# Opening the feed-forward stage's pools ahead of the last residual, and computing two of its early products there

## The chip, the cores and the metric

The kernel runs on one core of a Trainium2 chip. The metric is the device time of one execution in microseconds (us), taken as the median of several executions. All work is in float32; TensorE is fed with float32r operands.

## The reference, cut to what matters

One diffusion block over 512 latent tokens of width 1024 (with 256 context tokens that only feed the scan). The change lies where the first half of the block ends and the second begins:

```python
mix = branch_merge(h, o_lat, z, sc_p, fn_u, ..., w_gate, b_gate, w_o)   # ends in merged @ w_o
x = x + g1 * mix
x = x + g2 * swiglu(modulate(x, norm2_g, sh2, sc2), w_ffn_in, w_ffn_out)
return rmsnorm(x, final_g)

def rmsnorm(t, gain):
    return t * rsqrt(mean(t * t, axis=-1) + 1e-6) * gain
def modulate(t, gain, shift, scale):
    return rmsnorm(t, gain) * (1 + scale) + shift
def swiglu(h, w_ffn_in, w_ffn_out):
    a, b = split_cols(h @ w_ffn_in, (2816, 2816))
    return (silu(a) * b) @ w_ffn_out
```

`w_o` is 1024 x 1024, `w_ffn_in` 1024 x 5632, `w_ffn_out` 2816 x 1024. `setup_inputs()` draws all of them from normal distributions.

## The kernel before, in words

**Splitting.** A float32 operand is split into a high part (a rounding to float32r, on ScalarE, L143) and a low part (the rest, on VectorE, L144). Every product is then three matmuls: high by high, high by low, low by high. Weights come in pieces of 128 x 1024 elements (512 KB): `load_w` (L136) issues the DMA on SyncE's queue into the buffer `wf` (three of them), `prep_w` (L146) splits the piece into `wh` and `wl` (two of each), or into tiles that are handed in as `dst`.

**The `w_o` product** (`gemm_tm`, L975) keeps four token tiles `m` of 128 tokens in eight PSUM banks. The first weights go through all four tiles; the last four pieces (three of them split into `ex0`, `ex1`, `ex2`, one held in `wh`/`wl`) are kept, and with them the tiles are finished one after the other. As each tile is done, the loop at L1059 adds it to the stream `xr` (`residual`, L1002: an addition on VectorE for each 512 columns, a square with a sum on ScalarE, a square root and a reciprocal), scales it to `xn` (L1061), transposes it on TensorE (eight 128 x 128 transposes, L1071), and applies gain and shift (L1075, L1077).

**The feed-forward input** `h @ w_ffn_in` is done in 2 x 2 blocks with seven products instead of eight (a Strassen scheme). The normed tokens are the blocks B11, B21 (tokens 0 to 255, the two halves of the contraction) and B12, B22 (tokens 256 to 511); `sums_b` (L1038) makes from them T1, T2, T3 and minus B22, and L1140 makes T4. They lie, split, in `ob` (and `obt`, `ob4`). The 2816 columns go in 11 groups `g` of 256. In a group, one `prod` (L1101) is 24 matmuls of 256 columns. Weights for the seven products are single pieces of `w_ffn_in` or sums of pieces: two of the sums are made by the DMA itself, which loads one piece (`load_w2`, SyncE's queue) and accumulates another onto it (`acc_w`, GpSimd's queue); in the list of a group these are `t` and `w`. The next sums are made on VectorE (`add_w`, L1115).

For the first three groups the two products that only need B11 and B21 are taken ahead of the loop (`ahead`, `ahead2`, L1124 to L1139), so that TensorE has work while T1 to T4 are still being made. In order, TensorE does: B11 by the pieces of groups 0, 1, 2; B21 by the pieces of groups 0, 1, 2; then, for each group, T1, T2, T3, minus B22, T4 (and B11, B21 from group 3 on).

**What sets the order.** The program is written as Python and a scheduler puts the instructions of each engine in a row by priority; each engine works its row in order. Loads and splits under `prio("prep")` stand as early as their place in the row allows. A tile waits for the last use of whatever lay in its memory. Pools open and close as a stack: `pF` (L810) serves the stage before and holds, among others, the tiles of the norm (`xn`, `h2f`, `tb`); `pG` (L1089), the pool of the feed-forward stage with `ws`, `Gq`, `tmps`, opens where `pF` closes, after the last residual. The sum `w` of every group lies in `ws`, the sum `t` in one of two places in `c16` (`pre`). Two of the three results of the early products are kept in `e01`, which is one of the three `wf` buffers (L1134).

Of the kernel before, what the change touches and what calls it, by code (L numbers as in the profile page):

```python
# [74 lines left out]
def body(tc, I, out):  # L75
# [3 lines left out]
    with es:  # L79
# [806 lines left out]
        uus = [pF.tile([128, 512], F32, name="uu", tag=t_, bufs=2) for t_ in ("u", "u", "gt", "gt")]  # L886
        for t_, p_ in zip(uus, pus[0] + pu2):
            A.copy(out=t_, in_=p_)
        def fourier(g):
            uu = uus[g]  # L890
            eo = pF.tile([128, 2, 256], F32, name="eo", tag="eo", bufs=2)
            V.tensor_tensor(out=eo[:, 0], in0=uu[:, 1:257], in1=uu[:, 511:255:-1], op=ALU.add)
            V.tensor_tensor(out=eo[:, 1], in0=uu[:, 1:257], in1=uu[:, 511:255:-1], op=ALU.subtract)
            up = pF.tile([128, 2, 2, 2, 128], F32R, name="up", tag="dng" if g % 2 else "up")
# [26 lines left out]
        for j2 in range(4):  # L921
            gt = [pF.tile([128, 512], F32, name="gt", tag="gt", bufs=2) for _ in range(2)]
# [6 lines left out]
        dnh = [pF.tile([128, 4, 512], F32, name="dng", tag=t_) for t_ in ("up", "dng")]  # L929
# [95 lines left out]
        xn = pF.tile([128, 2, 1024], F32, name="xn", tag="dng")  # L1025
# [33 lines left out]
        for m, ps in gemm_tm(I["w_o"][0], g1b, lambda k, ms: (mh[:, k, ms], ml[:, k, ms]), 8, extra, 1):  # L1059
            rs_ = residual(ps, xr, m, [xn[:, m % 2, 512 * n:512 * n + 512] for n in range(2)])  # L1060
# [3 lines left out]
            for k4 in range(2):  # L1064
                px = dbank()
                p3 = px.rearrange("p (k j) -> p k j", k=4)
                h3 = Bf[:, 4 * k4:4 * k4 + 4, js] if m < 2 else pF.tile([128, 512], F32, name="h2f", tag=("u", "gt")[m - 2], bufs=2).rearrange("p (k j) -> p k j", k=4)
# [16 lines left out]
        fstack.close()  # L1084
# [4 lines left out]
        pG = es.enter_context(tc.tile_pool(name="pG", bufs=1))  # L1089
        OB["T4"] = pG.tile([128, 2, 4, 256], F32R, name="ob4")  # L1090
        tmps = pG.tile([128, 7, 512], F32, name="tmps")
        e1g, e5, u2, e57, c22, c21, c12 = (tmps[:, i] for i in range(7))
        Gq = [pG.tile([128, 2, 512], F32, name="Gq", tag=f"Gq{i}") for i in range(11)]
        ws = [pG.tile([128, 4, 256], F32, name="ws", tag=f"ws{i}") for i in range(2)]
        third = [pG.tile([128, 4, 256], F32R, name="w3", tag=f"w3{i}") for i in range(2)]
        turn = itertools.count()
        prep3 = lambda w_: prep_w(w_, dst=third if next(turn) % 3 == 2 else None)
        wfi = I["w_ffn_in"][0].rearrange("(k p) f -> p k f", p=128)
        wsrc = lambda i, half, g: wfi[:, 4 * half:4 * half + 4, 2816 * i + 256 * g:2816 * i + 256 * g + 256]

        def prod(bank, w, b, first, last):  # L1101

            for q in range(2):
                o, cs = bank[:, 256 * q:256 * q + 256], slice(128 * q, 128 * q + 128)
                for kk in range(4):
                    mm = ((w[0], b[:, 0]), (w[0], b[:, 1]), (w[1], b[:, 0]))
                    for i, (l_, r_) in enumerate(mm):
                        T.matmul(o, lhsT=l_[:, kk, cs], rhs=r_[:, kk], start=first and q == kk == i == 0,  # L1108
                                 stop=last and kk == 3 and i == 2, skip_group_check=True)

        def acc_w(w, src):
            with prio("prep"):
                GP.dma_start(out=w, in_=src, accum_op=ALU.add)

        def add_w(w, other):  # L1115
            with prio("prep"):
                V.tensor_tensor(out=w, in0=w, in1=other, op=ALU.add)  # L1117
# [101 lines left out]
```

## Time and profile before

| | |
|---|---|
| median of the three runs shown | 964.57 us (960.88 to 968.45) |
| the profiled execution | 965.04 us |
| its span, first to last instruction | 963.2 us |
| TensorE busy | 939.9 us, 98% of the span |
| VectorE, ScalarE busy | 649.3 us, 467.9 us |
| last `w_o` matmuls to the regular rhythm of the groups | about 599.3 to 648.2 us of the span |

Times in the rows are microseconds from the start of the span. In a row of the timeline the columns are start, duration, engine, line, operation, output and inputs with shapes, count, and in brackets the idle time of the engine just before and what ended it. PE is TensorE's matmuls, DVE VectorE, ACT ScalarE, POOL GpSimd, SPq and POOLq the queues that issue DMAs. TensorE's operations overlap, so the duration of a row is longer than the step from one to the next.

### The profile page before, as it was taken

What the parts mean: (1) busy time and instruction counts of PE and PEld (TensorE: products, weight loads), DVE (VectorE), ACT (ScalarE), POOL (GpSimd) and SP (SyncE); (2) the same over time, 40 slices, a digit from 0 to 9 for tenths busy, and PEclk for the clock granted to TensorE, in tenths of its full rate; (3) what the DMA queues carried; (4) which work ended last, traced back from release to release, by engine and by line L of the source; (5) the groups of instructions that cost most, each with busy time, mean ns of one, the idle gap of its engine ahead of it and who ended that gap; (6) DMA issues with size and microseconds to landing.
All of it is one profiled execution on the core that took longest, in us unless ns stands there. A gap on an engine that the chain in (4) does not pass through costs nothing.

```text
span 963.2 us, 16357 instructions
## 1 busy us (share of the span) xinstructions
PE 939.9 (98%) x6660; PEld 807.7 (84%) x6660; DVE 649.3 (67%) x1002; ACT 467.9 (49%) x793; POOL 57.2 (6%) x69
## 2 busy tenths in 40 slices
PE   8999999999999999999999999799999999999997
PEld 7588887777788888888888888699999999988885
DVE  2585888378755423788874876778777777855575
ACT  5354885687673334362234336644444444422334
POOL 1002300000000000000000010112111110000000
PEclk9999999999999999999999999899999999999999
DMA  9920653521202232837774471689887774333332
GB/s 319 307 66 3 146 131 88 133 67 34 67 2 66 88 110 66 310 109 256 264 247 141 127 194 42 160 217 262 180 195 190 185 187 104 117 88 109 89 88 87
DMA packets 117434, 135.84 MB, mean 141 GB/s; under 512 B 18748, under 2 KB 104624, under 8 KB 117360
## 3 DMA queue, kind: packets, MB, share of 16 engines
q1 hardware_dynamic: 97168, 117.93, 39.2%
q0 software_dynamic: 13248, 14.98, 9.5%
q10 hardware_dynamic: 6944, 1.91, 0.8%
q8 instruction: 52, 0.85, 0.4%
q14 instruction: 22, 0.18, 0.1%
HBM read 131.02 MB, written 3.77 MB: 140 GB/s over the span
## 4 chain that ended last, share of the span: by engine, by line
PE 76%; DVE 9%; DMA 6%; ACT 6%; issue 2%; POOL 0%; SPq 0%; DVEq 0%; ACTq 0%
PE g L1108 17%; PE g L256 10%; PE g L257 10%; PE g L255 10%; PE d L256 5%; PE d L255 5%; PE d L257 5%; PE d L1108 3%; DVE wl L144 2%; DMA wm<-in_w_mod_dram 2%; DMA ws<-in_w_ffn_in_dram 1%; DVE acc L835 1%; DMA wf<-in_w_o_dram 1%; ACT wh L143 1%; ACT SJ L718 1%
## 5 line engine op out<-in xcount | busy, mean ns | idle before, releaser
L144 DVE TENSOR_TENSOR wl<-wf,wh 128x1024 fp32r<-128x1024 f32 x114 | 139.1, 1222 | 93.1 <-ACT wh L143 92.2
L143 ACT CAST wh<-wf 128x1024 fp32r<-128x1024 f32 x114 | 119.6, 1050 | 161.1 <-PE g L256 98.2
L255 PE MATMUL g<-hh,wh 128*128 128x512 f32 x368 | 145.6, 396 | 0.0
L257 PE MATMUL g<-hh,wl 128*128 128x512 f32 x368 | 145.3, 395 | 0.1
L256 PE MATMUL g<-hl,wh 128*128 128x512 f32 x368 | 145.2, 395 | 0.0
L1108 PE MATMUL g<-ob,wh 128*128 128x256 f32 x640 | 118.7, 287 | 3.8 <-ACT wh L143 3.8
L1108 PEld LDWEIGHTS g<-ob,wh 128*128 128x128 f32 x640 | 101.6, 195 | 4.5 <-ACT wh L143 4.5
L1108 PE MATMUL g<-ob,wl 128*128 128x256 f32 x320 | 91.6, 287 | 0.5 <-DVE wl L144 0.5
L257 PEld LDWEIGHTS g<-hh,wl 128*128 128x128 f32 x368 | 69.2, 188 | 14.5 <-issue 0.5
L256 PEld LDWEIGHTS g<-hl,wh 128*128 128x128 f32 x368 | 69.2, 188 | 13.6 <-issue 0.2
L255 PEld LDWEIGHTS g<-hh,wh 128*128 128x128 f32 x368 | 69.2, 188 | 13.6 <-issue 0.2
L1108 PEld LDWEIGHTS g<-ob,wl 128*128 128x128 f32 x320 | 62.3, 195 | 0.8 <-DVE wl L144 0.8
L835 DVE SCALAR_TENSOR_TENSOR acc<-wm,ct,acc 128x1024 f32<-128x1024 f32 x32 | 41.0, 1282 | 14.7 <-DMA acc<-in_b_mod_dram 7.6
L1108 PE MATMUL g<-ob,w 128*128 128x256 f32 x360 | 45.9, 283 | 0.2 <-issue 0.2
L1108 PEld LDWEIGHTS g<-ob,w 128*128 128x128 f32 x360 | 44.3, 192 | 0.4 <-issue 0.4
L143 ACT CAST gs<-Gq 128x512 fp32r<-128x512 f32 x22 | 13.4, 622 | 63.5 <-PE d L256 63.5
L143 ACT CAST wh<-c 128x1024 fp32r<-128x1024 f32 x21 | 22.0, 1048 | 37.0 <-DVE c L1117 19.5
L144 DVE TENSOR_TENSOR gs<-Gq,gs 128x512 fp32r<-128x512 f32 x22 | 15.0, 690 | 29.1 <-ACT gs L143 29.1
L154 DVE TENSOR_TENSOR wf<-wf,g2b 128x1024 f32<-128x1024 f32 x22 | 26.9, 1222 | 8.5 <-DMA wf<-in_w_ffn_out_dram 8.5
L255 PE MATMUL d<-wh,gs 128*128 128x512 f32 x80 | 31.1, 389 | 0.0
L257 PE MATMUL d<-wh,gs 128*128 128x512 f32 x80 | 31.1, 389 | 0.0
L256 PE MATMUL d<-wl,gs 128*128 128x512 f32 x80 | 31.1, 389 | 0.0
(481 smaller groups left out, 2078.3 us busy)
## 6 DMA issues: line engine op xcount, KB each, us to landing
wm<-in_w_mod_dram SPq DMA_DIRECT2D x48, 512.0 KB, 5.7
wf<-in_w_ffn_in_dram SPq DMA_DIRECT2D x39, 512.0 KB, 4.8
wf<-in_w_in_dram SPq DMA_DIRECT2D x31, 512.0 KB, 3.8
wf<-in_w_gate_dram SPq DMA_DIRECT2D x24, 512.0 KB, 3.8
wf<-in_w_ffn_out_dram SPq DMA_DIRECT2D x22, 512.0 KB, 3.6
c<-in_w_ffn_in_dram SPq DMA_DIRECT2D x11, 512.0 KB, 6.3
c<-in_w_ffn_in_dram POOLq DMA_DIRECT2D x11, 512.0 KB, 6.6
ws<-in_w_ffn_in_dram SPq DMA_DIRECT2D x11, 512.0 KB, 3.8
```

The source lines that it names most:

```text
L143: A.copy(out=hi, in_=f)
L144: V.tensor_tensor(out=lo, in0=f, in1=hi.bitcast(F32), op=ALU.subtract)
L154: V.tensor_tensor(out=w, in0=w, in1=scale, op=ALU.mult)
L255: T.matmul(ps, lhsT=lh, rhs=rh, start=start, stop=False)
L256: T.matmul(ps, lhsT=lh, rhs=rl, start=False, stop=False)
L257: T.matmul(ps, lhsT=ll, rhs=rh, start=False, stop=stop)
L718: A.activation(out=S[:, u ^ par, h], in_=S[:, u ^ par, h], func=AF.Copy, scale=eGl[:, u, c_:c_ + 1])
L835: V.scalar_tensor_tensor(out=acc, in0=w, scalar=ct[:, k, 0:1], in1=acc, op0=ALU.mult, op1=ALU.add)
L1108: T.matmul(o, lhsT=l_[:, kk, cs], rhs=r_[:, kk], start=first and q == kk == i == 0, stop=last and kk == 3 and i == 2, skip_group_check=True)
```

## The change

- The tiles of the second norm and of the step before it (`xn`, `h2f`, `tb`, and `uu`, `eo`, `gt`, half of `dng`) move from `pF` to a pool of their own, `pE`, on the other side of the memory.
- With these out of `pF`, `pF` closes and `pG` opens inside the loop over the `w_o` tiles, when the matmuls of the last tile (m = 3) have been written down and before its residual.
- At that place the first two early products (B11 by the pieces of groups 0 and 1) are written down, ahead of the last residual. The weights of group 0 go to `wh`/`wl`; those of group 1 are split into the place of minus B22 in `ob`, which is written only later in `sums_b`. The early result of group 2 stays behind the loop.
- The early results are kept in `tmps` (nine slices in place of seven); `e01` is gone.
- Group 0's two sums are both made in `pre`, which is loaded well ahead. From then on even groups have both sums in `pre`, odd groups both in `ws`. Before, `t` was in `pre` and `w` in `ws` for all groups.
- `pE` closes after the loop; `pG2` opens in its place for the last three `Gq` tiles and `third`.

```diff
+        estack = ExitStack()
+        pE = estack.enter_context(tc.tile_pool(name="pE", bufs=1, side="right"))
...
-        xn = pF.tile([128, 2, 1024], F32, name="xn", tag="dng")
+        xn = pE.tile([128, 2, 1024], F32, name="xn", tag="dng")
...
+        def sums_w(g, lower, left):
+
+            load_w2(wsrc(1, 0, g), lower)
+            acc_w(lower, wsrc(1, 1, g))
+            load_w2(wsrc(0, 0, g), left)
+            acc_w(left, wsrc(1, 0, g))
+
+        sums_w(0, *pre)
...
         for m, ps in gemm_tm(I["w_o"][0], g1b, lambda k, ms: (mh[:, k, ms], ml[:, k, ms]), 8, extra, 1):
+            if m == 3:
+
+                fstack.close()
+                pG = es.enter_context(tc.tile_pool(name="pG", bufs=1))
+                OB["T4"] = pG.tile([128, 2, 4, 256], F32R, name="ob4")
+                tmps = pG.tile([128, 9, 512], F32, name="tmps")
+                ws = [pG.tile([128, 4, 256], F32, name="ws", tag=f"ws{i}") for i in range(2)]
+                Gq = [pG.tile([128, 2, 512], F32, name="Gq", tag=f"Gq{i}") for i in range(8)]
+
+                Xs = [gbank() for _ in range(2)]
+                for g, dst in enumerate((None, (OB["nB22"][:, 0], OB["nB22"][:, 1]))):
+                    prod(Xs[g], prep_w(load_w(wsrc(0, 0, g)), dst=dst), OB["B11"], True, False)
             rs_ = residual(ps, xr, m, [xn[:, m % 2, 512 * n:512 * n + 512] for n in range(2)])
...
-        fstack.close()
-        pG = es.enter_context(tc.tile_pool(name="pG", bufs=1))
...
+        estack.close()
+        pG2 = es.enter_context(tc.tile_pool(name="pG2", bufs=1, side="right"))
+        Gq += [pG2.tile([128, 2, 512], F32, name="Gq", tag=f"Gq{i}") for i in range(8, 11)]
+        third = [pG2.tile([128, 4, 256], F32R, name="w3", tag=f"w3{i}") for i in range(2)]
...
-        e01 = stg.tile([128, 4, 256], F32, name="e01", tag="wf", bufs=3).rearrange("p a b -> p (a b)")
-        e1s = [e01[:, 0:512], e01[:, 512:1024], e1g]
+        e1a, e1b, e1g, e5, u2, e57, c22, c21, c12 = (tmps[:, i] for i in range(9))
+        e1s = [e1a, e1b, e1g]
         EARLY = 3
-        Xs = [ahead(g, e1s[g]) for g in range(EARLY)]
+        for g in range(2):
+            A.copy(out=e1s[g], in_=Xs[g])
+        Xs.append(gbank())
+        prod(Xs[2], prep_w(load_w(wsrc(0, 0, 2))), OB["B11"], True, False)
+        A.copy(out=e1s[2], in_=Xs[2])
...
         for g in range(11):
-            t, w = pre[g % 2], ws[g % 2]
-            load_w2(wsrc(1, 0, g), t)
-            acc_w(t, wsrc(1, 1, g))
-            load_w2(wsrc(0, 0, g), w)
-            acc_w(w, wsrc(1, 0, g))
+            t, w = (pre, ws)[g % 2]
+            if g:
+                sums_w(g, t, w)
```

What stands in an engine's row moves as follows. Up to the first residual nothing moves on any engine. ScalarE's row just ahead of the residual of tile m = 0, before (`wh` is the high part of the last `w_o` piece and of group 0's piece; the two `xn` rows are the squares of the residual):

```order
L143 CAST ex_5306<-wf 128x1024
L143 CAST ex_5308<-wf 128x1024
L143 CAST wh<-wf 128x1024 x2
L1009 ACTIVATE xn,n_s<-xr 128x512 x2
L1011 ACT_TABLE_LOAD
L1011 ACTIVATE n_r<-n_r,eps 128x1
```

and now (`ob` is the place of minus B22, `wf` here group 1's piece):

```order
L143 CAST ex_5309<-wf 128x1024
L143 CAST ex_5311<-wf 128x1024
L143 CAST wh<-wf 128x1024 x2
L143 CAST ob<-wf 128x1024
L1011 ACTIVATE xn,n_s<-xr 128x512 x2
L1013 ACT_TABLE_LOAD
L1013 ACTIVATE n_r<-n_r,eps 128x1
```

One cast has come in ahead of the first residual, and on VectorE likewise its low part, ahead of the first two additions to `xr`.

TensorE's row at the end of the `w_o` product, where the transposes of tile m = 3 stand (`cp`, `xn`), before, with buffer numbers (`g_5735` and `g_5767` are the banks of groups 0 and 1, `ob_5311` holds B11):

```order
L1108 MATMUL g_5735<-ob_5311,wh_5738 128x256 x2
L1108 MATMUL g_5735<-ob_5311,wl_5739 128x256
L1071 MATMUL d_5669<-cp_82,xn_5310 128x128 x4
L1071 MATMUL d_5679<-cp_82,xn_5310 128x128 x4
L1108 MATMUL g_5767<-ob_5311,wh_5770 128x256 x2
L1108 MATMUL g_5767<-ob_5311,wl_5771 128x256
```

and now (`g_5682`, `g_5683`, `g_5807` are the banks of groups 0, 1 and 2, `ob_5315` holds group 1's weights):

```order
L1047 MATMUL g_5682<-ob_5314,wh_5686 128x256 x2
L1047 MATMUL g_5682<-ob_5314,wl_5687 128x256
L1047 MATMUL g_5683<-ob_5314,ob_5315 128x256 x24
L1116 MATMUL d_5752<-cp_82,xn_5313 128x128 x4
L1116 MATMUL d_5762<-cp_82,xn_5313 128x128 x4
L1047 MATMUL g_5807<-ob_5314,wh_5810 128x256 x2
L1047 MATMUL g_5807<-ob_5314,wl_5811 128x256
```

Group 1's product of 24 matmuls has moved from behind the transposes to ahead of them.

VectorE's row ahead of T2 of group 0, before (`c_5314` is `c16`, `w_5732` and `w_5733` are `third`; the row `c<-c,wf` is the first `add_w`):

```order
L144 TENSOR_TENSOR wl<-wf,wh 128x1024
L144 TENSOR_TENSOR wl<-c_5314,wh 128x1024
L144 TENSOR_TENSOR w_5733<-ws,w_5732 128x1024
L1117 TENSOR_TENSOR c_5314<-c_5314,wf 128x1024
L144 TENSOR_TENSOR wl<-c_5314,wh 128x1024
```

and now:

```order
L1156 TENSOR_TENSOR c_5317<-c_5317 128x1024
L144 TENSOR_TENSOR wl<-c_5317,wh 128x1024
L144 TENSOR_TENSOR w_5804<-c_5317,w_5803 128x1024
L1141 TENSOR_TENSOR c_5317<-c_5317,wf 128x1024
L144 TENSOR_TENSOR obt<-c_5317,obt 128x4x128
```

The split of group 0's sum `w`, which stands ahead of the `add_w`, reads `c16` now, where it read `ws`.

More of the change, by code (lines that the diff above doesn't have):

```diff
@@ L885, in body @@
         (pu2,) = gemm_fm(win[:, :, 3856:4112], ((LAT[0], LAT[1], 512, dbank),))
-        uus = [pF.tile([128, 512], F32, name="uu", tag=t_, bufs=2) for t_ in ("u", "u", "gt", "gt")]
+        uus = [pE.tile([128, 512], F32, name="uu", tag=t_, bufs=2) for t_ in ("u", "u", "gt", "gt")]
         for t_, p_ in zip(uus, pus[0] + pu2):
@@ L921, in body @@
         for j2 in range(4):
-            gt = [pF.tile([128, 512], F32, name="gt", tag="gt", bufs=2) for _ in range(2)]
+            gt = [pE.tile([128, 512], F32, name="gt", tag="gt", bufs=2) for _ in range(2)]
             gate(2, j2, gt)
@@ L928, in body @@
             tick(5)
-        dnh = [pF.tile([128, 4, 512], F32, name="dng", tag=t_) for t_ in ("up", "dng")]
+        dnh = [p_.tile([128, 4, 512], F32, name="dng", tag=t_) for p_, t_ in ((pF, "up"), (pE, "dng"))]
         dng = [dnh[j // 4][:, j % 4] for j in range(8)]
@@ L1033, in body, with prod, acc_w, load_w2 @@
         OB = {"B11": ob[0][:, 0], "B21": ob[0][:, 1], "nB22": ob[1][:, 0], "T3": ob[1][:, 1], "T1": ob[2][:, 0], "T2": ob[2][:, 1]}
+        wfi = I["w_ffn_in"][0].rearrange("(k p) f -> p k f", p=128)
+        wsrc = lambda i, half, g: wfi[:, 4 * half:4 * half + 4, 2816 * i + 256 * g:2816 * i + 256 * g + 256]
+        def prod(bank, w, b, first, last):
+            for q in range(2):
+                o, cs = bank[:, 256 * q:256 * q + 256], slice(128 * q, 128 * q + 128)
+                for kk in range(4):
+                    mm = ((w[0], b[:, 0]), (w[0], b[:, 1]), (w[1], b[:, 0]))
+                    for i, (l_, r_) in enumerate(mm):
+                        T.matmul(o, lhsT=l_[:, kk, cs], rhs=r_[:, kk], start=first and q == kk == i == 0,
+                                 stop=last and kk == 3 and i == 2, skip_group_check=True)
+        def acc_w(w, src):
+            with prio("prep"):
+                GP.dma_start(out=w, in_=src, accum_op=ALU.add)
+        def load_w2(src, w):
+            with prio("prep"):
+                SY.dma_start(out=w, in_=src)
+            return w
+        def sums_w(g, lower, left):
[4 more added lines that the diff above has]
+        sums_w(0, *pre)
         def split_b(f, name, js):
@@ L1066, in body @@
                 p3 = px.rearrange("p (k j) -> p k j", k=4)
-                h3 = Bf[:, 4 * k4:4 * k4 + 4, js] if m < 2 else pF.tile([128, 512], F32, name="h2f", tag=("u", "gt")[m - 2], bufs=2).rearrange("p (k j) -> p k j", k=4)
+                h3 = Bf[:, 4 * k4:4 * k4 + 4, js] if m < 2 else pE.tile([128, 512], F32, name="h2f", tag=("u", "gt")[m - 2], bufs=2).rearrange("p (k j) -> p k j", k=4)
                 hs.append(h3)
```

34 lines of the change are left out of this document (3 added, 31 removed).

## The prediction

> **What bounds the kernel now.** I read the page's busy table first, then the table by stretches around the change, then TensorE's waits there, then the chain of waits.
>
> ```profile
> span 963.2 us, 16357 instructions
> PE 939.9 (98%) x6660; PEld 807.7 (84%) x6660; DVE 649.3 (67%) x1002; ACT 467.9 (49%) x793; POOL 57.2 (6%) x69
> ```
>
> TensorE is the bound, and the change removes no matmul. What it can win is the time in which TensorE stands or runs slowly around the edited place, no more. The columns of the next view are the stretch, its length, the busy time and count of PE, PEld, DVE, ACT and POOL, the granted TensorE clock, the DMA share, and GB/s.
>
> ```profile
> 575.00:599.26 24.26, 24.20 (x118) 19.58 (x117) 16.39 (x35) 14.29 (x35) 0.00 (x0) 1.00 0.14 44
> 599.26:648.17 48.91, 41.63 (x299) 39.70 (x298) 36.67 (x47) 26.98 (x41) 5.12 (x4) 0.90 0.68 176
> 648.17:662.57 14.40, 14.40 (x122) 14.40 (x122) 12.70 (x15) 6.26 (x8) 2.56 (x2) 1.00 1.04 269
> 629.50:632.90 3.40, 2.09 (x13) 1.50 (x13) 2.20 (x3) 1.53 (x2) 0.00 (x0) 1.00 0.80 247
> 632.90:636.30 3.40, 3.40 (x18) 3.40 (x18) 2.03 (x2) 1.04 (x1) 1.27 (x1) 0.50 0.58 158
> 240.40:243.80 3.40, 1.79 (x15) 1.12 (x15) 3.40 (x9) 2.41 (x8) 0.00 (x0) 1.00 0.01 2
> ```
>
> The first row is the end of the `w_o` product and the third the regular rhythm of the groups: in both TensorE is full, at full clock. The second row, between them, is not. The waits of TensorE inside it (in all, times, longest), the transposes, and two pieces of the chain (start, length, what):
>
> ```profile
> PE g L1108 <- ACT wh L143: 4.3, 4, 2.1
> PE d L1071 <- DVE xn L1061: 1.2, 1, 1.2
> PE d L1108 <- ACT wh L143: 1.0, 1, 1.0
> PE g L1108 <- DVE wl L144: 0.5, 1, 0.5
> ...
> 603.54 1.06 PE L1071 MATMUL d<-cp,xn 128*128 128x128 f32 x8 [1.25 <-DVE xn L1061]
> ...
> 599.47 0.69 DVE xr L1008
> ...
> 648.17 2.88 PE d L1108 x24
> ```
>
> One product of 24 matmuls takes 2.88 us. From the last `w_o` matmul to 648.17, where T2 of group 1 begins, TensorE has twelve: B11 and B21 for three groups, five of group 0, and T1 of group 1. With the transposes that is 12 x 2.88 + 1.06 = 35.62 us of work in 48.91 us, so **13.29 us are lost**: 48.91 - 41.63 = 7.28 us standing (the four waits are 7.0 of it), and the rest in matmuls that ran slowly, at a mean clock of 0.90. The cause reads off the waits: behind `w_o` there is one product ready, then xn of tile 3 is waited for, then the split weights of the next early products, for which `wh` and `wl` have only two places each and `wf`, with `e01` in it, two left.
>
> **The change part by part.** *Taken away.* Two products, 5.76 us of TensorE work, now stand ahead of the transposes of tile 3, with weights split ahead of tile 0, and all three `wf` buffers serve. The wait for xn and the early waits for `wh`, `wl` (1.2 + 4.3 + 0.5 = 6.0 us) lose their cause, and so does the slow stretch that follows them. xn of tile 3 is ready at 602.65 + 0.75 = 603.4 in the row below, 4.1 us behind the end of `w_o`; the two products cover 5.76. Slack 1.6 us.
>
> The wait of 1.0 us and the half clock behind it come from the sum `w` of group 0:
>
> ```profile
> 614.84 0.92 SPq L1121 DMA_DIRECT2D ws<-in_w_ffn_in_dram  x2
> ...
> 619.50 2.58 POOL L1113 DMA_DIRECT2D ws<-in_w_ffn_in_dram  x2 [60.39 <-DMA ws<-in_w_ffn_in_dram]
> ...
> 626.61 1.05 ACT L143 CAST w<-ws 128x1024 fp32r<-128x1024 f32 x1 [2.30 <-DMA ws<-in_w_ffn_in_dram]
> ...
> 627.69 1.23 DVE L144 TENSOR_TENSOR w<-ws,w 128x1024 fp32r<-128x1024 f32 x1 [1.93 <-ACT w L143]
> 628.84 1.22 DVE L1117 TENSOR_TENSOR c<-c,wf 128x1024 f32<-128x1024 f32 x1
> ...
> 630.14 1.04 ACT L143 CAST wh<-c 128x1024 fp32r<-128x1024 f32 x1 [1.50 <-DVE c L1117]
> ...
> 631.24 0.50 PE L1108 MATMUL d<-obt,wh 128*128 128x256 f32 x2 [1.03 <-ACT wh L143]
> ```
>
> `ws` can be loaded only once `pG` has its memory; from 614.84 every step to TensorE at 631.24 waits for the one before. Group 0's `w` now lies in `c16`, loaded long before, so this chain goes. `ws` serves group 1 from then on; its loads wait for the last `w_o` matmul instead of 614.84, so they start about 14 us earlier, and are needed about 11 us earlier. Nothing is lost there.
>
> If everything came in time, all 13.29 us would go. Two things take some of it back.
>
> *s, a stall added at tile 0.* Group 1's cast and low part now stand on ScalarE and VectorE ahead of the first residual. Behind them are queued the additions to `xr`, the squares, xn, and for these waits TensorE:
>
> ```profile
> 573.98 2.00 ACT L143 CAST wh<-wf 128x1024 fp32r<-128x1024 f32 x2 [1.75 <-DVE wf L154]
> 578.06 0.63 ACT L1009 ACTIVATE xn<-xr 128x512 f32<-128x512 f32 x1 [2.08 <-DVE xr L1008]
> ...
> 573.79 1.22 DVE L144 TENSOR_TENSOR ex<-wf,ex 128x1024 fp32r<-128x1024 f32 x1
> 575.07 2.36 DVE L144 TENSOR_TENSOR wl<-wf,wh 128x1024 fp32r<-128x1024 f32 x2
> 577.34 0.68 DVE L1008 TENSOR_TENSOR xr<-xr,g 128x512 f32<-128x512 f32 x1
> 579.88 0.69 DVE L1008 TENSOR_TENSOR xr<-xr,d 128x512 f32<-128x512 f32 x1 [1.86 <-PE d L257]
> ...
> 583.99 0.39 PE L256 MATMUL d<-ex,mh 128*128 128x512 f32 x1
> 584.30 0.63 PE L1071 MATMUL d<-cp,xn 128*128 128x128 f32 x4
> ```
>
> and the times from issue to landing of pieces of 512 KB, around 607, 568, 577 and 654 us:
>
> ```profile
> wf<-in_w_ffn_in_dram SPq DMA_DIRECT2D x1, 512.0 KB, 3.4
> ...
> wf<-in_w_o_dram SPq DMA_DIRECT2D x1, 512.0 KB, 3.7
> ...
> wf<-in_w_ffn_in_dram SPq DMA_DIRECT2D x1, 512.0 KB, 4.8
> ...
> wf<-in_w_ffn_in_dram SPq DMA_DIRECT2D x1, 512.0 KB, 9.3
> ```
>
> Group 1's piece goes into the buffer that the `ex` row leaves at 573.79 + 1.22 = 575.0. It lands 3.4 to 3.7 later (the two rows in the nearest traffic), near 578.6. Cast 1.05: 579.65. Low part, by the step of the two `wl` rows (2.27 / 2 = 1.14): 580.8. The first addition takes 0.6, so the second starts near 581.4 in place of 579.88: 1.5 us late. The transposes of 584.30 stand right behind a matmul of 583.99, with no slack, so TensorE stands these 1.5 us, and tiles 1 to 3 move with it. I take s = 1.5. Ends: 0.5, if the transposes had a us of slack that the rows don't show, and 2.7 with the landing of 4.8.
>
> *w, VectorE ahead of T2 of group 0.* With TensorE dense, VectorE's work between the last residual and the first `add_w` has to fit under it. Its steps:
>
> ```profile
> 602.65 0.75 DVE L1061 TENSOR_SCALAR xn<-xr,n_r 128x1024 f32<-128x1024 f32 x1
> 603.31 0.68 DVE L1047 TENSOR_TENSOR c<-h2f,c 128x512 f32<-128x512 f32 x1
> 603.91 0.68 DVE L144 TENSOR_TENSOR ob<-tb,ob 128x512 fp32r<-128x512 f32 x1
> 604.52 0.72 DVE L1077 TENSOR_SCALAR h2f<-d,a,sh 128x128 f32<-128x128 f32 x2
> 605.16 0.68 DVE L144 TENSOR_TENSOR obt<-c,obt 128x512 fp32r<-128x512 f32 x1
> ```
>
> A pass over 512 columns steps by 0.60, a pair of gains by 0.64, xn by 0.66, a pass over 1024 by 1.14. In VectorE's row of the changed kernel, from the last addition to `xr` to the first `add_w`, stand 14 passes of 512 (8.4), 8 of 1024 (9.1), xn (0.66), two pairs (1.28) and some columns (0.2): 19.7 us. The addition starts 0.2 behind the last `w_o` matmul (599.47 against 599.26), and the cast behind the `add_w` is 1.05: 20.9 us. TensorE has seven products and the transposes by then, 7 x 2.88 + 1.06 = 21.2 us. Balanced: 0.3 us to spare if VectorE never waits. But it follows ScalarE in places, as the row of 627.69 does. I take w = 0.5, between 0 and 3 (three waits of 1 us, about what it stood in that row, half again).
>
> The other edits have one answer. The new wait of ScalarE's high part of minus B22 on group 1's product ends before ScalarE gets to it (both near 605.5), and behind it stand only copies of early results with room for over 2 us. The copies themselves are as many as before. The pools' sides move memory, not work.
>
> *Sum.* 13.29 - 1.5 - 0.5 = 11.3 us. The profiled execution is 965.04 us: 953.7. The median of the runs shown, 964.57, lies 0.47 lower: **953.3 us**, 1.2% less. About 1%, 9.6 us, is what a measurement of this kernel can tell from no change: faster means below 954.9.
>
> **The rivals.** *Half clock at tile 0* (R1). The row 632.90:636.30 shows half the clock, 1.7 us lost, right after a stretch, 629.50:632.90, in which TensorE was busy for 2.09 of 3.40 us, with waits of only about 1.3. A stall of 1.5 us could bring the same. Against it: 240.40:243.80, busy for 1.79 only, kept the full clock. It gives 955.0.
>
> The Trainium skill, "TensorE: Matmul & The Clock Gate", section "Part 1: The HAM clock gate (the "warmup" mystery)", has the clock fall only after an idle window of some 3.4 us. By it the stall costs its own 1.5 us and the sum stays; the row of 632.90 speaks against that rule, the row of 240.40 for it.
>
> *VectorE paces* (R2). If the waits for ScalarE add up, w is 2.5 to 5: 955.3 to 957.8, say 956.5. For it: 0.3 us of spare; against it: ScalarE is busy for 26.98 of 48.91 us.
>
> *DMA paces* (R3). 648.17:662.57 has a DMA share of 1.04 at 269 GB/s with TensorE still full. If the groups now start on less store of loaded pieces, groups 1 and 2 wait perhaps 1 us each, and a third for a late `ws`: 956. Against it: the loads move ahead by more than the need.
>
> *The gain is given back* (R4): a later stage waits for something with its own pace, and the time stays at 964 to 965. Nothing after 648.17 in the rows shows such a wait.
>
> *Slower* (R5): group 1's piece lands late. ScalarE and VectorE work in order, so every us of landing beyond 3.55 stops tile 0, and with it TensorE, for a us. With the 9.3 us of the last landing row s is 1.5 + 5.75 = 7.25, half clock adds 1.7, and the gain is 13.29 - 7.25 - 1.7 - 0.5 = 3.8. The sign turns at 9.3 + 3.8 = 13 us; at 16 us, which takes a queue busy with several pieces ahead of it, the time is 967.5. For it: the piece stands in SyncE's queue behind other loads. Against it: the DMA share in 575.00:599.26 is 0.14.
>
> **How the numbers follow.** Forecast, 0.60: 951.3 (s and w at nothing) to 955.4 (s 2.7, w 1.4). R1 0.10, R2 0.12, R3 0.06, R4 0.07, R5 0.05. The range reaches from 950.5, a little under that lower end, to 960.0: this takes in R1, R2, R3 and the milder half of R5, and leaves out R4 and the rest of R5. Faster by over 1%: the forecast without its upper twentieth, and a few hundredths of R1 and R2, 0.60. Slower by over 1%, beyond 974, needs a landing over 20 us: 0.02. Within 1%: 0.38.
>
> **What would show it right or wrong.** Right: a TensorE wait of 1 to 2 us for xn near 584, and none of over 0.5 us from the end of `w_o` to T2 of group 0; a granted clock of 1.00 there; the stretch from the last `w_o` matmul to T2 of group 1 at 36 to 37 us in place of 48.91. Each term is wrong by itself if: the wait near 584 is below 0.5 or above 2.7 (s); TensorE waits over 1.4 us for `wh` at T2 of group 0 (w); the clock reads 0.5 after 584 (R1); waits for `ws` or `wf` appear in groups 1 to 3 (R3). The forecast as a whole falls if that stretch is down by 11 us or more and the span is not.

## The result, and the profile after

The changed kernel takes **952.54 us** (median of four runs, 951.71 to 956.95) against 964.78 us before; the ratio is 0.9887, 95% interval 0.9853 to 0.9920. The forecast was 953.3 us. The profiled execution took 951.71 us, 13.33 us less than the one of before.

The busy table of the changed kernel:

```profile
span 949.8 us, 16357 instructions
PE 931.6 (98%) x6660; PEld 800.9 (84%) x6660; DVE 648.4 (68%) x1002; ACT 468.3 (49%) x793; POOL 57.2 (6%) x69
```

The same number of instructions; TensorE is busy 8.3 us less: 6.1 of them in the stretch of the second row below (41.63 against 35.53), part of which ran at half clock before, and 1.6 in the groups behind it. Its stretches, in the columns of the prediction: the end of the `w_o` product, the stretch from there to T2 of group 1, the first regular group, and the 3.42 us around tile 0's transposes.

```profile
575.00:601.07 26.07, 24.84 (x120) 20.06 (x120) 18.13 (x36) 15.73 (x36) 0.00 (x0) 1.00 0.27 82
601.07:636.60 35.53, 35.53 (x297) 35.36 (x296) 34.08 (x45) 26.07 (x39) 5.13 (x4) 1.00 0.88 224
636.60:650.92 14.32, 14.32 (x123) 14.32 (x121) 13.07 (x16) 6.38 (x7) 2.56 (x2) 1.00 1.08 244
...
583.79:587.21 3.42, 2.25 (x13) 1.66 (x12) 1.73 (x4) 1.82 (x4) 0.00 (x0) 1.00 0.32 106
```

The second row answers to the 48.91 us of before: 35.53 us, full, at full clock. The first row is new: TensorE stands 26.07 - 24.84 = 1.23 us in it, where it stood for 0.06. The waits of TensorE between 560 and 700 us, and the two places where it waited:

```profile
PE g L256 <- DVE wl L144: 1.4, 1, 1.4
PE d L1116 <- DVE xn L1106: 1.2, 1, 1.2
...
569.45 0.50 PE L256 MATMUL g<-wl,mh 128*128 128x512 f32 x1 [1.41 <-DVE wl L144]
...
586.14 0.63 PE L1116 MATMUL d<-cp,xn 128*128 128x128 f32 x4 [1.17 <-DVE xn L1106]
```

The second is the stall s. The first is a piece of `w_o` that came late; in the kernels below it lies between nothing and 1.3 us, at 1.3 in one (`f4_wf_alone`) in which nothing changes there, so I count it as scatter. The row of before:

```profile
568.86 0.50 PE L256 MATMUL g<-wl,mh 128*128 128x512 f32 x1 [0.27 <-DVE wl L144]
```

To add up, I take the starts of four matmuls in each trace: the last but one of the stage before `w_o`, the last of `w_o`, and the first of T2 of group 1 and of group 10.

| stretch | before | after | difference |
|---|---|---|---|
| start to the end of the stage before `w_o` | 551.42 | 550.88 | -0.54 |
| from there to the last matmul of `w_o` | 47.62 | 49.97 | +2.35 |
| from there to T2 of group 1 | 48.97 | 35.76 | -13.21 |
| T2 of group 1 to T2 of group 10 | 172.80 | 171.20 | -1.60 |
| from there to the end | 142.43 | 142.04 | -0.39 |
| span | 963.23 | 949.84 | -13.39 |

Three of these are the change: -13.21, the stall in the second row (1.17 of its 2.35; 1.13 is the late piece of `w_o`, 1.41 against 0.27), and -1.60, of which the prediction says nothing. In the experiments below I use the time from the end of the stage before `w_o` to T2 of group 1, less the wait for the piece of `w_o`; call it **the passage**. It is 47.62 + 48.97 - 0.27 = 96.3 us before and 49.97 + 35.76 - 1.41 = 84.3 after.

### The profile page after: what moved, and what is told of

Read it like the earlier page. It is cut to its first block, busy times and chain, and to the rows that moved or that the text cites. A ratio compares the mean times of both kernels' runs of the same rounds, so it can differ in the third digit from the quotient of the medians.

```text
span 949.8 us, 16357 instructions
## 1 busy us (share of the span) xinstructions
PE 931.6 (98%) x6660; PEld 800.9 (84%) x6660; DVE 648.4 (68%) x1002; ACT 468.3 (49%) x793; POOL 57.2 (6%) x69
## 4 chain that ended last, share of the span: by engine, by line
PE 78%; DVE 8%; DMA 7%; ACT 5%; issue 2%; POOL 0%; SPq 0%; DVEq 0%; ACTq 0%
PE g L1047 19%; PE g L255 10%; PE g L256 10%; PE g L257 10%; PE d L255 5%; PE d L256 5%; PE d L257 5%; PE d L1047 3%; DMA wm<-in_w_mod_dram 2%; DVE wl L144 2%; DMA wf<-in_w_o_dram 2%; DVE acc L837 1%; PE t L255 1%; PE t L257 1%; PE t L256 1%
## 5 line engine op out<-in xcount | busy, mean ns | idle before, releaser
L143 ACT CAST wh<-wf 128x1024 fp32r<-128x1024 f32 x113 | 118.7, 1050 | 159.0 <-PE g L256 95.2
L1047 PE MATMUL g<-ob,wh 128*128 128x256 f32 x624 | 113.4, 283 | 0.0
L1047 PEld LDWEIGHTS g<-ob,wh 128*128 128x128 f32 x624 | 97.2, 192 | 0.1
L1047 PE MATMUL g<-ob,wl 128*128 128x256 f32 x312 | 88.2, 283 | 0.0
L1047 PEld LDWEIGHTS g<-ob,wl 128*128 128x128 f32 x312 | 59.8, 192 | 0.0
L143 ACT CAST wh<-c 128x1024 fp32r<-128x1024 f32 x17 | 17.9, 1050 | 22.5 <-DVE c L1141 10.4
```

The costliest lines, as they stand in the source:

```text
L143: A.copy(out=hi, in_=f)
```

## The experiments

All times are medians, the ratios are against the kernel before, run beside each on the same chip.

| kernel | time, us | ratio (95%) | xn wait at tile 0 | passage | nine groups |
|---|---|---|---|---|---|
| before | 964.78 | 1 | 0 | 96.3 | 172.80 |
| changed | 952.54 | 0.9887 (0.9853-0.9920) | 1.17 | 84.3 | 171.20 |
| `e1_late_split` | 952.11 | 0.9867 (0.9827-0.9906) | 0 | 83.5 | 171.20 |
| `e2_one_ahead` | 953.58 | 0.9883 (0.9846-0.9919) | 0 | 84.4 | 171.20 |
| `e3_sums_as_before` | 953.44 | 0.9879 (0.9842-0.9916) | 1.20 | 84.3 | 171.20 |
| `e4_third_aligned` | 952.79 | 0.9876 (0.9844-0.9909) | 1.14 | 84.3 | 171.99 |
| `f1_e01_in_wf` | 956.98 | 0.9929 (0.9906-0.9952) | 1.3 | 90.0 | 171.20 |
| `f3_pools_alone` | 961.11 | 0.9985 (0.9965-1.0004) | 0 | 92.7 | 171.20 |
| `f4_wf_alone` | 964.36 | 0.9997 (0.9972-1.0022) | 0 | 94.4 | 172.80 |
| `f5_pools_and_wf` | 952.55 | 0.9884 (0.9859-0.9909) | 0 | 83.9 | 171.20 |
| `e5_weights_shifted` | 959.85 | 0.9958 (0.9941-0.9974) | 0.13 | 83.6 | 170.13 |
| `g1_ffn_shift` | 953.58 | 0.9890 (0.9864-0.9916) | 1.2 | 84.5 | 168.43 |
| `g2_both` | 952.98 | 0.9889 (0.9865-0.9913) | 0 | 83.7 | 168.45 |
| `g3_shift_packed` | 949.07 | 0.9857 (0.9831-0.9882) | 0 | 83.5 | 168.00 |

The last two columns are read from one trace each; they part kernels that the medians, which scatter by 2 to 7 us, do not.

### Is the stall at tile 0 the early split?

```diff
-                for g, dst in enumerate((None, (OB["nB22"][:, 0], OB["nB22"][:, 1]))):
-                    prod(Xs[g], prep_w(load_w(wsrc(0, 0, g)), dst=dst), OB["B11"], True, False)
+                for g in range(2):
+                    prod(Xs[g], early[g], OB["B11"], True, False)
...
+            if m == 0:
+                early = [prep_w(load_w(wsrc(0, 0, 0))), (OB["nB22"][:, 0], OB["nB22"][:, 1])]
+                A.copy(out=early[1][0][:, 0, 0:1], in_=rs_)
+                split(load_w(wsrc(0, 0, 1)), *early[1])
```

> Edit: group 1's early weights are still loaded ahead, but their split is tied behind tile 0's residual (a one-column copy of that residual's reciprocal into the same place, which the split then overwrites). Theory (the stall s comes from this split standing ahead of tile 0 on ScalarE and VectorE): TensorE's wait of 1.17 us for xn near 586 disappears, the time is 1 to 1.5 us below the changed kernel's, and the early product of group 1 still starts without a wait. Rival (the place of the split is of no account, TensorE waits there for the chain of the residual itself): a wait of about 1 us at the first transposes remains, the time is that of the changed kernel. Second rival (the low part, 1.2 us of VectorE, now delays tile 1): a wait of about 1 us appears at a later tile's transposes.

Yes, that wait is gone. The changed kernel's ScalarE and VectorE around group 1's split:

```profile
579.12 1.05 ACT L143 CAST ob<-wf 128x1024 fp32r<-128x1024 f32 x1 [1.17 <-DMA wf<-in_w_ffn_in_dram]
...
580.21 1.22 DVE L144 TENSOR_TENSOR ob<-wf,ob 128x1024 fp32r<-128x1024 f32 x1 [1.00 <-ACT ob L143]
581.35 0.68 DVE L1010 TENSOR_TENSOR xr<-xr,g 128x512 f32<-128x512 f32 x1
581.95 0.68 DVE L1010 TENSOR_TENSOR xr<-xr,d 128x512 f32<-128x512 f32 x1
```

and ScalarE with the split tied behind the residual:

```profile
587.72 0.17 ACT L1127 CAST ob<-n_r 128x1 fp32r<-128x1 f32 x1
587.92 1.05 ACT L143 CAST ob<-wf 128x1024 fp32r<-128x1024 f32 x1
```

In the first, the additions to `xr` stand behind a load; in the second the cast comes when tile 0 is through, and TensorE waits for no xn. The passage is 0.8 us shorter, not 1.17: TensorE comes sooner to T1 of group 0, the product ahead of T2, and a wait of 0.4 us is new there:

```profile
621.99 0.38 PE L1047 MATMUL g<-obt,wl 128*128 128x256 f32 x1 [0.36 <-DVE wl L144]
```

(The scheduler also moved tile 2's transposes behind the end of `w_o`, which shifts 1 us from one half of the passage to the other.) In the medians 0.8 us is not to be seen. How long the stall is hangs on when the piece lands and when TensorE gets to the transposes: in `e5_weights_shifted`, below, the split stands as in the changed kernel and the wait is 0.13 us.

### Are two products ahead, and the sums in c16, what wins?

```diff
-                for g, dst in enumerate((None, (OB["nB22"][:, 0], OB["nB22"][:, 1]))):
-                    prod(Xs[g], prep_w(load_w(wsrc(0, 0, g)), dst=dst), OB["B11"], True, False)
+                prod(Xs[0], prep_w(load_w(wsrc(0, 0, 0))), OB["B11"], True, False)
...
+        prod(Xs[1], prep_w(load_w(wsrc(0, 0, 1))), OB["B11"], True, False)
```

> Edit: only group 0's early product is written ahead of the last residual; group 1's goes back behind the loop, with its weights in wh and wl; pools, sums and places as in the changed kernel. Theory (two products, 5.76 us, are what covers the 4.1 us until xn of tile 3; one, 2.88 us, does not): TensorE waits about 1.2 us for xn of tile 3, and up to 2 us more for the split weights of group 1; the stall of 1.2 us at tile 0 is gone; in all 1 to 3 us slower than the changed kernel, more if the clock is halved there. Rival (the open pool alone, with three wf places and tmps for the early results, brings the gain): no wait of over 0.5 us, the time 1 us below the changed kernel's.

Neither came out. There was no wait for xn of tile 3 and no stall at tile 0, but one wait for `wl`, late, in T1 of group 0:

```profile
620.96 0.38 PE L1047 MATMUL g<-obt,wl 128*128 128x256 f32 x1 [1.07 <-DVE wl L144]
```

What the expectation had wrong is where group 1's product stands. Written behind the loop, it still comes ahead of the transposes of tile 3 in TensorE's row: all of group 1 and eleven matmuls of group 2 are there. That the scheduler does so because it sees their weights ready early is likely, but not shown. So early writing is not what puts it ahead. The 1.1 us balance the missing stall, and the passage is that of the changed kernel.

The sums:

```diff
-        sums_w(0, *pre)
...
-            t, w = (pre, ws)[g % 2]
-            if g:
-                sums_w(g, t, w)
+            t, w = pre[g % 2], ws[g % 2]
+            sums_w(g, t, w)
```

> Edit: the sums go back to their old places (t in the two places of c16, w in ws, for every group), everything else as in the changed kernel. Theory A (as the prediction had it: group 0's w in c16, loaded long before, is what removes the wait of 1.0 us ahead of T2 of group 0): a wait of about 1 us, and perhaps half clock behind it, returns there; 1 to 3 us slower than the changed kernel. Theory B (the pool that opens early is enough: ws is loaded from about 601 on, its chain to TensorE took 16.4 us before, so it is done near 618, and T2 starts near 622): no wait, the time that of the changed kernel within 0.5 us.

Theory B came out. With group 0's `w` back in `ws`, SyncE and ScalarE did this:

```profile
604.60 0.92 SPq L1056 DMA_DIRECT2D ws<-in_w_ffn_in_dram  x2
...
620.74 1.05 ACT L143 CAST w<-ws 128x1024 fp32r<-128x1024 f32 x1
```

`ws` is loaded 0.2 us after the end of `w_o`, where before the load waited until 614.84, and the cast no longer waits for it. TensorE has no wait there, and the passage is 84.3 us as in the changed kernel. Moving the sums to `c16` bought nothing that the free memory under `ws` did not buy already.

### What wins, then?

Four kernels take the two remaining parts away, alone and together: the norm's tiles apart from the next stage's memory (pools), and the third `wf` buffer, which the early results held (`wf`).

In the first the changed kernel gives the third `wf` buffer back to the early results:

```diff
-        e1s = [e1a, e1b, e1g]
+        e01 = stg.tile([128, 4, 256], F32, name="e01", tag="wf", bufs=3).rearrange("p a b -> p (a b)")
+        e1s = [e01[:, 0:512], e01[:, 512:1024], e1g]
```

> Edit: the changed kernel, but the early results of groups 0 and 1 are kept in one of the three wf buffers again, as before. Theory (two early products ahead of the residual, with weights in nB22's place, are enough): TensorE full from the end of w_o to T2 of group 1 as in the changed kernel, 35.8 us for that stretch, same time. Rival (the third wf buffer is what lets the split weights of the next products come in time): waits for wh or wl of 2 to 4 us there, and with them half clock; 3 to 6 us slower than the changed kernel.

The rival came out. Both products are written ahead, and yet the weights of the next ones are late. TensorE's waits in the stretch, and its clock in two windows:

```profile
608.22 0.50 PE L1047 MATMUL g<-ob,wh 128*128 128x256 f32 x2 [1.56 <-ACT wh L143]
609.48 0.39 PE L1047 MATMUL g<-ob,wl 128*128 128x256 f32 x1 [0.76 <-DVE wl L144]
617.70 0.39 PE L1047 MATMUL g<-ob,wl 128*128 128x256 f32 x1 [0.71 <-DVE wl L144]
...
607.26:610.67 3.41, 1.69 (x12) 1.49 (x13) 2.47 (x4) 3.38 (x7) 0.03 (x1) 1.00 1.20 201
610.67:614.08 3.41, 3.41 (x19) 3.41 (x18) 3.38 (x6) 1.59 (x3) 0.00 (x0) 0.50 1.16 250
```

These are 3.03 us of waits and 1.7 us of half clock. The passage is 5.7 us longer than with the buffer; the remaining 1.0 us I have not traced.

The pools alone, in the kernel before (the other tiles of the norm likewise, and `third` and three of the `Gq` in `pG2`):

```diff
-        xn = pF.tile([128, 2, 1024], F32, name="xn", tag="dng")
+        xn = pE.tile([128, 2, 1024], F32, name="xn", tag="dng")
...
+        estack.close()
+        pG2 = es.enter_context(tc.tile_pool(name="pG2", bufs=1, side="right"))
```

> Edit: the kernel before with the pools alone changed: the norm's tiles in a pool of their own on the right, so that ws and the other tiles of the next stage lie where nothing of the norm lies. The products stay behind the residual, the early results in wf, the sums where they were. Theory (ws loaded from about 600 on is what ends the wait ahead of T2 of group 0): the wait of 1.0 us and the half clock of 1.7 us behind it are gone, the waits for xn and wh of 6 us remain with their half clock; 2.5 to 4 us below the kernel before, of which 1.6 come from the third places lying elsewhere. Rival (those waits move as a whole): the loss stays at 13 us and the time is that of the kernel before less 1.6.

As the theory had it, the wait at T2 of group 0 is gone, and those for xn and `wh` stay.

```profile
602.52 1.06 PE L1102 MATMUL d<-cp,xn 128*128 128x128 f32 x8 [1.26 <-DVE xn L1092]
606.55 0.80 PE L1047 MATMUL g<-ob,wh 128*128 128x256 f32 x2 [2.97 <-ACT wh L143]
```

In this trace the passage falls by 3.6 us and the groups by 1.6. The medians show less: 5.2 us would be a ratio of 0.9946, which lies below the interval of 0.9965 to 1.0004. The traced execution, 958.82 us, is the fastest of ten; the median is 961.11, and that the time falls at all is not certain.

The buffer alone, in the kernel before:

```diff
-        e01 = stg.tile([128, 4, 256], F32, name="e01", tag="wf", bufs=3).rearrange("p a b -> p (a b)")
+        e01 = pG.tile([128, 4, 256], F32, name="e01", tag="e01").rearrange("p a b -> p (a b)")
```

> Edit: the kernel before with one line changed: the early results of groups 0 and 1 are kept in 4 KB of the next stage's own pool in place of one of the three wf buffers. In TensorE's row group 1's product then stands ahead of the transposes of tile 3, as in the changed kernel. Theory (the two products ahead are what covers xn; no early writing and no pool is needed for that): the wait for xn and most of those for wh go, 6 to 10 us below the kernel before; the wait ahead of T2 of group 0 remains or grows, since ws still comes late and TensorE is there sooner. Rival (the cover is not the point, the late ws is): what is won ahead is given back as a wait of 6 to 9 us ahead of T2 of group 0, and the time falls by 3 us at most.

The rival came out, in a place that neither theory named:

```profile
615.29 0.80 PE L1108 MATMUL g<-ob,wh 128*128 128x256 f32 x2 [7.07 <-ACT e L1128]
...
614.66 1.07 ACT L1128 COPY e<-g 128x512 f32<-128x512 f32 x2
```

Group 1's product does move ahead and the waits for xn and `wh` go. But now the early results must be copied into memory of the next stage's pool before B21 may be added in their banks, and the copy comes when the norm's tiles are done: 7.07 us. One wait replaced another, and the kernel is as fast as before.

Both together, still with nothing written ahead of the residual and with the sums as before (`f3_pools_alone` with this):

```diff
-        e01 = stg.tile([128, 4, 256], F32, name="e01", tag="wf", bufs=3).rearrange("p a b -> p (a b)")
-        e1s = [e01[:, 0:512], e01[:, 512:1024], e1g]
+        e1s = [e1a, e1b, e1g]
```

> Edit: the kernel before with two things of the change alone: the norm's tiles in their own pool, and the early results in the next stage's pool in place of a wf buffer. Nothing is written ahead of the last residual, the sums are where they were. Theory, after the runs so far (each of the two alone wins 2 to 3.6 us of the stretch, because the early results' place has to be free early for the wf buffer to be of use): the two together bring the stretch from the last w_o matmul to T2 of group 1 from 48.97 to 36 to 38 us, with no stall at tile 0; the time within 1 us of the changed kernel's. Rival (writing two products ahead of the residual is needed for the cover): the wait for xn of 1.3 us and waits for wh of 2 us and more remain, the stretch is 41 us or longer.

Together they give the whole gain, as the theory had it: a ratio of 0.9884, a passage of 83.9 us, no stall at tile 0, and one wait in the stretch, again in T1 of group 0:

```profile
620.18 0.39 PE L1047 MATMUL g<-obt,wl 128*128 128x256 f32 x1 [0.59 <-DVE wl L144]
```

So of the passage's 12.0 us, the pools alone are worth 3.6 and the buffer alone 1.9, together 12.4, in one trace each. The ratios say the same more sharply: 0.15% and 0.03% alone, neither clear of nothing, and 1.16% together, against 1.13% for the whole change. Writing the two products ahead of the residual and moving the sums add nothing to that; the one brings the stall at tile 0 and takes away a later wait of about the same size.

### Where do the 1.6 us in the groups come from?

In the chain of waits of both kernels TensorE runs alone through the groups. Before:

```profile
723.05 17.28 PE g L1108 x144
740.33 2.88 PE d L1108 x24
```

and after:

```profile
711.00 17.12 PE g L1047 x144
728.12 2.81 PE d L1047 x24
```

17.28 us for 144 is 120.0 ns each; 2.81 for 24 is 117.1. The starts of single matmuls show that all products fed from the two `third` places, and no others, go at 117 ns (116.8 from start to start inside a product). Of these 552 matmuls 480 lie between T2 of group 1 and T2 of group 10: 480 x 3.2 = 1.5 of the 1.60 us, and the rest lies in the steps at the ends of these products. What changed for them is their address.

```diff
         third = [pG2.tile([128, 4, 256], F32R, name="w3", tag=f"w3{i}") for i in range(2)]
+        pG2.tile([128, 24], F32, name="pad", tag="pad")
```

> Edit: 96 bytes of padding in the pool on the right, so that the third places for split weights start at a multiple of 128 bytes, as they did in the kernel before, and not 96 bytes past one. In the changed kernel the matmuls fed from these places follow each other at 117.2 ns, before at 120.0 ns, all others of that shape at 120 in both. Theory (the start address of the weights within 128 bytes sets this): back to 120.0 ns, 552 x 2.8 ns = 1.5 us slower than the changed kernel. Rival (the far end of the memory, or their being apart from the tokens' places, sets it): 117 ns as in the changed kernel and the same time.

The result lies between the two: 118.4 ns, nine groups in 171.99 us. The address counts, but its place within 128 bytes alone does not set the pace.

```diff
+        for n_, sh_ in (("wf", (3, F32)), ("padA", 8), ("wh", (2, F32R)), ("padB", 8), ("wl", (2, F32R)), ("padC", 16)):
+            if isinstance(sh_, int):
+                stg.tile([128, sh_], F32, name=n_, tag=n_)
...
```

> Edit: the changed kernel with 32 bytes of padding ahead of wh and 32 more ahead of wl, and 64 behind, so that wh lies 96 bytes, wl 64 bytes short of the tokens' places when counted within 128; the third places keep theirs. Theory (the distance of the weights' address from that of the tokens, taken within some power of two, sets the pace of matmuls of 256 columns): those fed from wh and wl go from 120 to between 117 and 119 ns too, 1,296 of them, 1 to 4 us below the changed kernel. Rival (the right end of the memory, as the last run's 118.5 ns at an aligned address allows): 120 ns as before, the same time. Second rival (other stages pay: matmuls of 512 columns or VectorE's passes get slower): their pace leaves 227 ns or 1.22 us.

The theory and its second rival came out at once: matmuls fed from `wh` and `wl` went from 120.0 to 118.3 (`wh`) and 117.0 ns (`wl`), and the kernel became slower than the changed one. The `third` places did not move in this run, but the tokens' places did, by the 128 bytes of padding, and the matmuls fed from `third` went from 116.8 to 118.7 ns: so it is not the weights' address by itself that counts. In the window 855 to 935 us, in the `w_ffn_out` product, TensorE is full in all kernels, and one counts the matmuls of 512 columns (second figure in brackets is PEld); the changed kernel, and then this one:

```profile
855.00:935.00 80.00, 80.00 (x353) 65.73 (x352) 48.15 (x54) 28.34 (x41) 0.00 (x0) 1.00 0.30 92
```

```profile
855.00:935.00 80.00, 80.00 (x346) 64.52 (x345) 46.82 (x47) 25.52 (x34) 0.00 (x0) 1.00 0.30 92
```

353 against 346: 226.6 and 231.2 ns. The page of the profile lists 1,104 matmuls of 512 columns in three rows of 368 alone, so this costs 1,104 x 4.6 ns = 5.1 us at least, where the nine groups win 1.1. VectorE's passes over 1024 columns stayed at 1.22 us.

The next two shift the weights in the `w_ffn_in` stage alone, the second with the split of `e1_late_split`.

```diff
-                    wh = stg.tile([128, 4, 256], F32R, name="wh", tag="wh", bufs=2)
-                    wl = stg.tile([128, 4, 256], F32R, name="wl", tag="wl", bufs=2)
+                    wh, wl = (stg.tile([128, s_], F32R, name=n_, tag=n_, bufs=2)[:, off:off + 1024].rearrange("p (a b) -> p a b", a=4) for n_, s_ in (("wh", 1056), ("wl", 1056)))
...
-        prep3 = lambda w_: prep_w(w_, dst=third if next(turn) % 3 == 2 else None)
+        prep3 = lambda w_: prep_w(w_, dst=third if next(turn) % 3 == 2 else None, off=24)
```

> Edit: the changed kernel, with wh and wl each 128 bytes longer, and split weights of the w_ffn_in stage alone written 96 bytes into them; all other stages use them from the start. Theory (matmuls of 256 columns gain where the weights' address is off the tokens' grid, those of 512 columns lose; so shift the one and not the other): those fed from wh and wl go from 120 ns to between 117 and 119, 1,296 of them, 1.5 to 3.6 us below the changed kernel, and those of 512 columns stay at 227 ns. Rival (it was the place of the tokens or of other tiles that moved them in the run before): 120 ns and no gain.

> Edit: the shift of the run before together with the split of group 1's early weights behind tile 0's residual. Theory (both gains stand by themselves): 0.8 us from the missing stall and 1.5 to 3.6 us from the pace, 2.3 to 4.4 us below the changed kernel, 948 to 950.5 us. Rival (the gain at tile 0 is given back as TensorE's wait ahead of T2 of group 0, 0.4 us when it was tried alone): 1.5 to 3.2 us below.

The first half came out: 117 to 118 ns for all products, nine groups in 168.4 us, as in this piece of the chain of `g1_ffn_shift`:

```profile
751.01 16.84 PE g L1046 x144
767.85 2.80 PE d L1046 x24
```

But the time did not fall, for the matmuls of 512 columns were slower again, 348 in the window:

```profile
855.00:935.00 80.00, 80.00 (x348) 65.04 (x347) 47.77 (x52) 27.63 (x40) 0.00 (x0) 1.00 0.30 91
```

The 128 bytes added to each of the four places had moved three of them off their old distance for the other stages too. So the four go into one piece without gaps:

```diff
+        wpk = stg.tile([128, 4224], F32R, name="wpk", tag="wpk")
...
+                    a = off + 1024 * (next(wturn) % 2)
+                    wh, wl = (wpk[:, c:c + 1024].rearrange("p (a b) -> p a b", a=4) for c in (a, a + 2048))
```

with an offset of 56 columns (224 bytes) in the `w_ffn_in` stage. In this kernel group 0's early piece, so shifted, runs over the first 56 columns of the low part of the last `w_o` piece, which tiles 1 to 3 still need, so that these are computed with weights that aren't theirs; the instructions of each engine and the transfers are as many as in `e1_late_split`. Leaving that one piece unshifted would part the two; this was not run, and the time below is that of a kernel which does not compute the block.

> Edit: group 1's early split tied behind tile 0's residual, and wh and wl (two of each) in one piece of memory without gaps; in the w_ffn_in stage the split weights are written 224 bytes into it, the distance that the third places have from the tokens' places within 512 bytes in the changed kernel; all other stages use it from its start, which is as far from the tokens' places as before. Theory (the distance within 512 bytes sets the pace: zero is best for 512 columns and worst for 256): 256 columns at 117 ns for all products, 512 columns at 227 ns, so 3.6 us from the pace and 0.8 us from the missing stall, 947 to 950 us. Rival (the distance counts by a larger power of two, or the gaps were not what slowed the 512 columns in the two runs before): 512 columns stay at 230 ns, 952 to 954 us.

The theory came out. The chain in the groups, and the window of the 512 columns:

```profile
767.90 16.80 PE g L1050 x144
784.70 2.80 PE d L1050 x24
...
855.00:935.00 80.00, 80.00 (x353) 65.97 (x352) 47.60 (x54) 28.55 (x43) 0.00 (x0) 1.00 0.29 92
```

That is 117 ns and 226.6 ns, and 949.07 us, 0.9857 of the kernel before. Its interval and the changed kernel's overlap; that it is faster than the changed kernel rests on the two stretches (0.8 and 3.2 us) and on a median 3.5 us lower, 2.3 us when each is taken against the kernel before on its own chip.

From the addresses in the built programs, the distance of the weights' place from the tokens' place, within 512 bytes, and the pace of the 256-column matmuls fed from there (the mean step from one start to the next inside a product):

| distance, bytes | 0 | 96 | 128 | 224 | 352 | 416 | 448 | 480 |
|---|---|---|---|---|---|---|---|---|
| pace, ns | 120.0 | 118.7 | 118.4 | 116.8 | | 118.3 | 117.0 | |
| in `g1_ffn_shift` | | 117.7 | | 116.7 | 117.1 | | | 116.5 |

At 96 bytes two kernels differ by 1.0 ns, so the distance is not the whole of it. For 512 columns, distance 0 gave 226.9 ns in the changed kernel, 256 gave 227.4 (`g1_ffn_shift`), and 128, 384, 416 and 448 gave 231 to 233. The pieces of the `w_ffn_out` product that are kept at distance 0 took 230.5 and 231.6 ns in `g1_ffn_shift` and `e5_weights_shifted`, where they alternate with shifted ones. That 512 is the period was assumed, and no run tested it by itself; a period of 256 fits as well, since 0 and 256 agree for 512 columns, and 224 and 480, 96 and 352 are within 0.6 ns of each other in `g1_ffn_shift`.

## Why the prediction was right, and where it was not

- **The loss of 13.29 us goes**: right, 13.21 measured. (The chain's piece starts at 648.17, the first matmul of T2 of group 1 at 648.00, so the prediction's sum is 0.17 us too large.) The sum by what TensorE has to do in that stretch needed no knowledge of which part of the change removes which wait. This carried the forecast.
- **s = 1.5**: right in its mechanism and near in size, 1.17 us. Cast, low part and additions came in the order foretold, the second addition at 581.95 where I had 581.4.
- **w = 0.5**: 0 measured, and the balance was as close as foretold. The cast behind the first `add_w` ends at 621.18 + 1.05 = 622.23, the first matmul of T2 starts at 622.29. Where the stall at tile 0 was taken away (`e1`, `e2`, `f5`), TensorE came sooner and did wait a product earlier, in T1 of group 0, for 0.4 to 1.1 us. The cast, and TensorE's first matmuls there:

```profile
621.18 1.05 ACT L143 CAST wh<-c 128x1024 fp32r<-128x1024 f32 x1 [0.25 <-DVE c L1141]
...
622.29 0.51 PE L1047 MATMUL d<-obt,wh 128*128 128x256 f32 x2
```

- **"Two products ... now stand ahead of the transposes of tile 3 ... The wait for xn and the early waits ... lose their cause"**: the effect was right, the cause was not. The written place is not needed (`e2`, `f5`); without the third `wf` buffer it does not suffice (`f1`, 5.7 us). The prediction named the buffer in half a sentence and priced it at nothing.
- **"Group 0's `w` now lies in `c16` ... so this chain goes"**: wrong cause. It goes because `ws` gets its memory 14 us earlier (`e3`). The prediction had that number, used it only to show that nothing is lost for group 1, and did not ask whether it would do for group 0 as well. The row of the changed kernel shows it: the chain of before, 16.4 us from 614.84 to 631.24, would from here end near 617.7, and T2 starts at 622.29.

```profile
601.30 0.92 SPq L1056 DMA_DIRECT2D ws<-in_w_ffn_in_dram  x2
```

- **"The pools' sides move memory, not work"**: wrong by 1.6 us, in the kernel's favour. This is the term that the sum put at nothing. By its own terms the sum comes to 13.21 - 1.17 + 1.60 = 13.6 us, where I had 11.3; the scatter in the other rows of the table takes 0.25 of that away. The profiled execution came out 2.0 us below the 953.7 that the prediction has for it; that the median lies only 0.8 us from the forecast is partly luck, since four executions of the changed kernel are spread over 5 us.
- **The rivals**: half clock at tile 0 (R1) did not come, VectorE did not pace (R2), the groups were not short of data (R3, third row of the table by stretches: full at a DMA share of 1.08), and nothing was given back (R4). Group 1's piece landed for the cast at 579.12, where I had 578.6, so R5 had no ground either.

## What to carry to other kernels

Count the work of the bound engine between two fixed points and forecast the loss as a whole; then, before crediting an edit with a wait, ask what else in the same change ends that wait, and try the parts alone and in pairs: here two cheap parts gave 0.03% and 0.15% alone and all of the gain together, and two elaborate ones nothing. A buffer freed is of use only when what it held has another place by then. Where a kernel is bound by matmuls, look at their pace from row to row before and after any change of a pool: some bytes of address were worth 1.6 us of the groups here, where the stall at tile 0 cost 1.2.

## What the runs showed of the hardware

**The pace of float32r matmuls depends on the addresses of the two operands against each other.** 256 columns: 120.0 ns at distance 0, 117 at 224 bytes; 512 columns the other way round, 227 at 0 and at 256 bytes and up to 233 elsewhere. The two cases differ in more than the columns: with 256 columns the weights are the operand that is loaded (LDWEIGHTS) and the tokens stream, in `w_o` and `w_ffn_out` it is the other way, and no run parts the two. The Trainium skill, "TensorE: Matmul & The Clock Gate", section "Step-by-step: what each phase is for", gives TensorE two read ports of its own for the two operands, so that loading weights takes nothing from a running matmul. These numbers do not agree with that in full: the operands' addresses against each other change the pace by 2 to 3%. What lies behind it, no run shows.

**The clock falls with a partly idle window, not only an idle one.** The half-clock stretches begin on a grid of 3.41 us (in the kernel before at 605.61 and 632.92, 8 x 3.41 apart). The window ahead of one had TensorE busy for 2.09 us of 3.40 (before, 629.50), 1.69 of 3.41 (`f1`, above), and here 0.79 (`f4_wf_alone`, with the 10.24 us at half clock that followed):

```profile
607.43:610.84 3.41, 0.79 (x7) 0.59 (x5) 3.31 (x6) 2.80 (x6) 0.00 (x0) 1.00 0.49 154
610.84:621.08 10.24, 5.79 (x27) 5.79 (x28) 6.31 (x9) 4.72 (x8) 2.09 (x2) 0.50 0.51 154
```

The window of the stall at tile 0, 583.79 to 587.21 after, had 2.25 of 3.42 and kept the clock. The rule of the Trainium skill, "TensorE: Matmul & The Clock Gate", section "Part 1: The HAM clock gate (the "warmup" mystery)", a fall after an idle window of 3.4 us, has the length right by these rows, and a window need not be idle for it. But the busy time that the profile shows is not the whole condition: the window of 240.40 in the prediction, on the same grid, had 1.79 and was not slowed, and in the changed kernel the window of 566.73, that of the late `w_o` piece, had 2.00 of 3.41 and kept the clock. What is counted stays open.
